# RWKV-7 layer and gated MLP on one core: TensorE's order fixed as emitted in the recurrent layer, and gram groups placed by direction

## The chip, the core and the metric

One core of a Trainium2 chip runs the whole program in one launch. The metric is the device time in microseconds of that execution; lower is better. Five engines matter: TensorE (PE in the profile) multiplies, VectorE (DVE) and ScalarE (ACT) do the elementwise work and empty TensorE's PSUM accumulators, GpSimd (POOL) does a few small operations, and SyncE (SP) issues the loads. Each engine runs its instructions in the order in which they stand in its program; an instruction waits, with all that stand behind it, until the semaphores of its inputs and buffers are set.

## The reference

Input x is 256 tokens of 2048 channels in float32. Two layers follow each other, each adding to its input, with a final norm:

```python
def rwkv7_bidir_mixer(h, ...):                     # layer 0; BRANCH = 4096, 64 heads of 64
    z = h @ w_in                                   # r, k, v, low-rank decay and rate, gate
    zs = zs + mu_prev*(shift_prev(zs)-zs) + mu_next*(shift_next(zs)-zs)
    kk = k*k_k / max(norm(k*k_k), 1e-12)           # per head
    for d, rev in ((0, False), (1, True)):         # two directions in time
        wll = -softplus(-(w0[d] + tanh(dw_d) @ w_up[d])) - 0.5
        decay = exp(-exp(wll))
        a_d = sigmoid(a0[d] + da_d @ a_up[d])
        k_d = k * (1 + (a_d - 1)*k_a)
        y += wkv_scan(r, decay, k_d, v, -kk, kk*a_d, rev)
        # S_t = S_{t-1} diag(w_t) + (S_{t-1} a_t) b_t^T + v_t k_t^T ;  y_t = S_t r_t
        bonus += sum(r*k_d*r_k) * v
    yn = group_norm(y)
    return ((yn + bonus) * silu(gate)) @ w_out

def chunked_sgu_mixer(z, ...):                     # layer 1
    u, v, gate = split(z @ w_in, 3)
    v = layer_norm(gelu(v)); s = w_s @ v (per chunk of 128 and group) + b_s
    return (gelu(u) * s * silu(gate)) @ w_out
```

The change concerns layer 0 alone.

## The kernel before

Each large product is taken in float32 precision by three passes over rounded halves: `mm3` multiplies the high half of the activations by the high half of the weights (line 161), the low half of the activations by the high half of the weights (162), and the high half by the low half (163). Names begin with `acc`; the weights come in 512 KB pieces `raw_*`, which ACT casts to `whi_*` (line 146) and from which DVE subtracts that (`wlo_*`, line 147). Three pieces at most are ahead.

Layer 0 is cut into 16 blocks `b` of two tiles of 128 channels, four heads. The work of a block is spread over three periods of a loop over `p`, and so each period holds work of three blocks:

- `mains(p)`: the projections. In the period of block b, k, r and the low-rank weights `wu` of block b, then v and g of block b-1: `acck`, `accr`, `accv`, `accg`, each 128 by 256 products.
- `factors(p)`: the norm of k (`hs`, line 385; `hb`, line 395; both TensorE), the low-rank products `up` (line 480), whose tanh copies ACT writes to TH and TA (line 482), the cumulated decay SS and its exponentials Et, and from them the factors of the chunked scan: BK (lines 531, 532) and AR (533, 535) on DVE, for both directions `d`, with 64 time steps per chunk, four chunks. `hs`, `hb` and `up` share one PSUM bank ("pf").
- `before(p-1)`: `grams`, the products of BK and AR within each chunk (`gp`, line 557). A gram group is the 8 products of one direction and one channel tile (two heads' halves h, four chunks c; 128 wide, 64 rows each); DVE masks its two banks ("pg", two of them) into Gs (line 562). Then `inverses`, the inverse of a triangular matrix per head and chunk: ACT lays out Dt and NQ (594, 595), DVE takes 31 steps in pairs (610, 612), TensorE makes `qp` (lines 624 and 630).
- `transposed_factors(p-1)`: `bp` (577).
- `after(p-2)`: `values` (`vp`, line 646, copied by ACT to SUV, and AR to RC at line 655), `chain`, four dependent steps i: `xp` and the output products of the state (684, 687), ACT's copy Xs (689), `uu` (693), ACT's copy SUV (695), `sp` and `yp` (700, 702), DVE's new state SJ (707 to 710), ACT's copy of it into SUV (712), which the next step's `xp` reads; last `finish` with the group norm (mv, rs, nm), the bonus `bb` and the transpose `yt` (747).

All these products are small, 64 columns wide or so, and lie between the 128 by 256 products of the projections.

Each of these functions is a generator. It yields the time within the period at which its next piece is to be emitted: a period is nominally `PERIOD` = 78, a step of the chain `CT` = 11 from 9 on, `TSUB` = 50 the end of the 31 steps, `TBT` = 36 the start of `bp`, `TUP` = 43 that of `up`. The loop at the end of the quoted code always advances the generator with the smallest time; that gives the order of emission. From it a scheduler makes the order on each engine: by its own estimates of when an instruction's inputs are there it may place later instructions ahead of earlier ones, and in this loop it does so on all engines. PSUM and SBUF buffers are handed out in emission order.

After the loop layer 0's rest (`oacc`, output projection) and layer 1 follow (`vacc`, `uacc`, `gacc`), which the change doesn't touch.

Of the kernel before, what the change touches and what calls it, by code (L numbers as in the profile page):

```python
# [10 lines left out]
F32 = mybir.dt.float32  # L11
F32R = mybir.dt.float32r
AF = mybir.ActivationFunctionType
ALU = mybir.AluOpType
# [8 lines left out]
def trunk(tc, x, norm_g, final_norm_g, w_in, mu_prev, mu_next, w0, w_up, a0, a_up, k_k, k_a, r_k,  # L23
          ln_w, ln_b, w_out, g_w_in, g_ln_g, g_ln_b, g_w_s, g_b_s, g_w_out, out):
    nc = tc.nc
    V, S, G, PE = nc.vector, nc.scalar, nc.gpsimd, nc.tensor
    P = 128
# [8 lines left out]
    C = 64  # L36
# [12 lines left out]
    raw_pools = [wp]  # L49
    RAW = 1024  # L50

    PERIOD, CT, TSUB, TBT, TEO, TUP = 78.0, 11.0, 50.0, 36.0, 1.2, 43.0
    EB, DK, LAST = 2, 4, 8
    psm = top.enter_context(tc.tile_pool(name="psm", bufs=1, space=PSUM))

    def sm(name, tag="pg", bufs=2):
        return psm.tile([P, 512], F32, tag=tag, name=name, bufs=bufs)
# [352 lines left out]


    MT = PERIOD / 16
    dt = 4 * MT / KT

    def mains(todo, st):
# [29 lines left out]
    def factors(b, f):  # L445
# [20 lines left out]

        PA = sc.tile([P, NC, 2, 2], F32, tag="PA", name=f"PA{b}", bufs=3)
        AR = sc.tile([P, 2, 2, NC, 2, C], F32, tag="AR", name=f"AR{b}", bufs=2)
        yield TUP
        _, wh, wl = f["wu"]  # L470
        ups = []
# [15 lines left out]
        for d in range(2):  # L487
            t = (TUP + 4, PERIOD * 0.7)[d]
            yield t
            th, ta = ups[d]  # L490

            S.activation(th, th, AF.Identity, bias=1.0)
            yield t + 1
            ss = fr.tile([P, 2 * T], F32, tag="SS", name=f"SS{b}_{d}")
            for cl in range(2):
                i0, i1, i2 = ss[:, cl * T:(cl + 1) * T], smask[:, d:d + T], th[:, cl]
                if d == 1:
                    i0, i1, i2 = i0[:, ::-1], i1[:, ::-1], i2[:, ::-1]
                V.tensor_tensor_scan(i0, i1, i2, 0.0, ALU.mult, ALU.add)
            yield t + 2  # L500
            et = fr.tile([P, 2, NC, C + 1], F32, tag="Et", name=f"Et{b}_{d}")
            ef = et.rearrange("p l c t -> p (l c) t")
            sv = ss.rearrange("p (c t) -> p c t", t=C)
            if d == 0:
                G.memset(ef[:, :, 0:1], 1.0)
                e_in, e_ex = ef[:, :, 1:C + 1], ef[:, :, 0:C]
            else:
                G.memset(ef[:, :, C:C + 1], 1.0)
                e_in, e_ex = ef[:, :, 0:C], ef[:, :, 1:C + 1]
            S.activation(e_in, sv, AF.Exp, scale=cE)  # L510
            S.activation(ss, ss, AF.Exp, scale=-cE)
            pe = et[:, :, :, C] if d == 0 else et[:, ::-1, ::-1, 0]
            G.tensor_copy(PA[:, :, d, :], pe.rearrange("p l c -> p c l"))
            yield t + 4

            for cl in range(2):
                j = cts[cl]
                S.activation(th[:, cl], ta[:, cl], AF.Identity, scale=kah[:, j:j + 1], bias=kab[:, j:j + 1])
            eng.tensor_tensor(th, th, Kt, ALU.mult)
            yield t + 6  # L520

            V.scalar_tensor_tensor(ta, ta, 1.0, NK, ALU.add, ALU.mult)

            if d == 0:
                yield PERIOD * 0.6
                BK = se.tile([P, 2, 2, NC, 2, C], F32, tag="BK", name=f"BK{b}")

            def slot(q, natural):
                return scan_order(BK[:, d].rearrange("p l c q t -> p (l c) q t")[:, :, q], d, natural)

            V.tensor_tensor(slot(0, False), tok(ta), sv, ALU.mult)
            eng.tensor_tensor(slot(1, True), tok(th), sv, ALU.mult)
            V.tensor_tensor(scan_order(AR[:, d, :, :, 0].rearrange("p l c t -> p (l c) t"), d), tok(NK), e_ex, ALU.mult)
            yield PERIOD * (0.63, 0.9)[d]
            V.tensor_tensor(scan_order(AR[:, d, :, :, 1].rearrange("p l c t -> p (l c) t"), d, True), tok(f["Rt"]), e_in,
                            ALU.mult)
            KD.append(th)
# [4 lines left out]
        for cl in range(2):  # L542
            V.scalar_tensor_tensor(BQ[:, cl], f["Rt"][:, cl], col["rk"][:, cts[cl]:cts[cl] + 1], KD[0][:, cl],
                                   ALU.mult, ALU.mult)
        f.update(PA=PA, AR=AR, BK=BK, BQ=BQ)

    def grams(b, f):

        AR, BK = f["AR"], f["BK"]
        Gs = sc.tile([P, 2, 16, 2 * C], F32, tag="Gs", name=f"Gs{b}", bufs=2)  # L550
        for d in range(2):
            for cl in range(2):

                gp = [sm(f"gp{b}_{h}{d}{cl}").rearrange("p (c q t) -> p c q t", c=NC, q=2) for h in range(2)]
                for c in range(NC):
                    for h in range(2):
                        PE.matmul(gp[h][:, c].rearrange("p q t -> p (q t)"),  # L557
                                  BK[H[h], d, cl, c].rearrange("p q t -> p (q t)"),
                                  AR[H[h], d, cl, c].rearrange("p q t -> p (q t)"), start=True, stop=True)
                u0 = (d * 2 + cl) * NC  # L560
                for h in range(2):
                    V.tensor_tensor(Gs[:, h, u0:u0 + NC], gp[h].rearrange("p c q t -> p c (q t)"),
                                    gmask[:, d].rearrange("p q t -> p (q t)").unsqueeze(1).to_broadcast([P, NC, 2 * C]),
                                    ALU.mult)
                yield 4 * (d * 2 + cl + 1)
        f["Gs"] = Gs

    def transposed_factors(b, f):
        yield TBT
# [12 lines left out]
    def inverses(b, f):  # L582
# [35 lines left out]
        qp = sm(f"qp{b}", "pq", 1).rearrange("p (u t) -> p u t", t=32)  # L618
        R0 = [slice(h * 64, h * 64 + 32) for h in range(2)]
        R1 = [slice(h * 64 + 32, h * 64 + 64) for h in range(2)]  # L620
        yield TSUB + 3
        for u in range(16):
            for h in range(2):
                PE.matmul(qp[R1[h], u], NQ[R0[h], u], Tn[R0[h], u], start=True, stop=True)
        for h in range(2):
            S.copy(NQ[R1[h]], qp[R1[h]])
        yield TSUB + 5
        for u in range(16):
            for h in range(2):
                PE.matmul(qp[R0[h], u], NQ[R1[h], u], TD[R1[h], u], start=True, stop=True)  # L630
        yield TSUB + 7
        for h in range(2):
            S.copy(TTs[R0[h], h, :, 32:64], qp[R0[h]])
            S.copy(TTs[R0[h], h, :, 0:32], TD[R0[h]])
# [23 lines left out]
    def chain(b, f):  # L658
# [17 lines left out]

        SJ = None
        for i in range(NC):
            t = 9 + CT * i
            yield t  # L680

            xp = part("xp", i)
            for d, l, h, u, suv in each(i):
                PE.matmul(xp[H[h], d * 2 + l], Gs[:, h, u, 0:C], suv, start=True, stop=True)
            if i > 0:
                for d, l, h, u, suv in each(i):
                    PE.matmul(y(d, l, h, i), RC[:, h, u], suv, start=False, stop=False, skip_group_check=True)
            Xs = sc.tile([P, 4, C], F32, tag="Xs", name=f"Xs{b}_{i}")
            S.copy(Xs, xp)
            yield t + CT * 0.27  # L690
            up = part("uu", i)
            for d, l, h, u, _ in each(i):
                PE.matmul(up[H[h], d * 2 + l], TTs[:, h, u], Xs[:, d * 2 + l], start=True, stop=True)
            for h in range(2):
                S.copy(SUV[H[0], :, :, i, h].rearrange("p d l v -> p (d l) v"), up[H[h]])
            yield t + CT * 0.54
            if i < NC - 1:
                sp = part("sp", i)
                for d, l, h, u, suv in each(i):
                    PE.matmul(sp[H[h], d * 2 + l], BT[:, h, u], suv, start=True, stop=True)  # L700
            for d, l, h, u, suv in each(i):
                PE.matmul(y(d, l, h, i), Gs[:, h, u, C:2 * C], suv, start=False, stop=False, skip_group_check=True)
            if i < NC - 1:
                Sn = sc.tile([P, 4, C], F32, tag="SJ", name=f"SJ{b}_{i}", bufs=2)
                pb = PA[:, i].rearrange("p d l -> p (d l)").unsqueeze(2).to_broadcast([P, 4, C])
                if i == 0:
                    V.tensor_tensor(Sn, sp, pb, ALU.mult)
                else:
                    V.tensor_tensor(Sn, sp, SJ, ALU.add)
                    V.tensor_tensor(Sn, Sn, pb, ALU.mult)  # L710
                for h in range(2):
                    S.copy(SUV[H[0], :, :, i + 1, h].rearrange("p d l v -> p (d l) v"), Sn[H[h]])
                SJ = Sn
        f["yp"] = yp

    def finish(b, f):

        tf = 9 + CT * 3.9
        yield tf
        yp, Vt = f["yp"], f["Vt"]  # L720
        st6 = sc.tile([P, 8, 6], F32, tag="st6", name=f"st6_{b}")
# [17 lines left out]
        PE.matmul(bb, ones2.rearrange("p h n -> p (h n)"), f["BQ"], start=True, stop=True)  # L739
        OT = sc.tile([P, 2, T], F32, tag="vy", name=f"OT{b}", bufs=2)  # L740
        V.tensor_tensor(OT, bb, Vt, ALU.mult)
        yield tf + 8
        yt = sm(f"yt{b}", "pc", 1).rearrange("p (l t) -> p l t", l=2)
        for cl in range(2):
            for c in range(NC):
# [10 lines left out]
        nc.scalar.dma_start(oT0[b * 2 * P:(b + 1) * 2 * P].rearrange("(l p) t -> p l t", p=P), OT)  # L756

    def before(b, f):
        yield from grams(b, f)
        yield from inverses(b, f)  # L760

    def after(b, f):
# [115 lines left out]
        oaccs["A"] = oA  # L878

    st = [{} for _ in range(NB)]  # L880
    for p in range(NB + 2):
        act = [mains(plan[p], st) if p <= NB else early_out()]
        if p == 0:
            act.append(low_rank())
        if p < NB:
            act.append(factors(p, st[p]))
        if 0 < p <= NB:
            act += [before(p - 1, st[p - 1]), transposed_factors(p - 1, st[p - 1])]
        if p > 1:
# [2 lines left out]
        while act:  # L892
            cur = min(act, key=lambda a: a[:2])
            try:
                cur[0] = max(cur[0], next(cur[2]))
            except StopIteration:
                act.remove(cur)
    ph.close()

    raw_pools.append(top.enter_context(tc.tile_pool(name="wp2", bufs=2, reuse_waits="tile")))  # L900
# [236 lines left out]
```

## Time and profile before

| | us |
|---|---|
| median of three runs | 2262.61 (2259.36 to 2264.06) |
| the profiled execution | 2260.96 |
| its span in the profile | 2259.2 |
| PE busy in the span | 2210.5 (98%) |
| DVE busy | 1601.3 (71%) |
| ACT busy | 1389.6 (62%) |
| POOL busy | 197.4 (9%) |
| loads | 339.36 MB, mean 150 GB/s |

The mean granted clock of TensorE is 0.992 of full speed. The recurrent layer's loop takes the first 1430 us of the span (the last `yt` starts at 1429.5); from block 4 on `acck` of one block starts 79.2 us after that of the block ahead. The three groups of `acck` products by line number 161, 162 and 163 hold 512 instructions each, 32 for each block. In the window rows each engine's busy time stands with its count of instructions, then the granted clock, the share of the DMA engines and the GB/s. In rows of the timeline the first number is the start, the second the time from the first start to the last end of that run of instructions, and in brackets stands the idle time before it and what ended that.

### The profile page before, as it was taken

What the parts mean: (1) busy time and instruction counts of PE and PEld (TensorE: products, weight loads), DVE (VectorE), ACT (ScalarE), POOL (GpSimd) and SP (SyncE); (2) the same over time, 40 slices, a digit from 0 to 9 for tenths busy, and PEclk for the clock granted to TensorE, in tenths of its full rate; (3) what the DMA queues carried; (4) which work ended last, traced back from release to release, by engine and by line L of the source; (5) the groups of instructions that cost most, each with busy time, mean ns of one, the idle gap of its engine ahead of it and who ended that gap; (6) DMA issues with size and microseconds to landing.
All of it is one profiled execution on the core that took longest, in us unless ns stands there. A gap on an engine that the chain in (4) does not pass through costs nothing.

```text
span 2259.2 us, 50510 instructions
## 1 busy us (share of the span) xinstructions
PE 2210.5 (98%) x21008; PEld 2013.8 (89%) x21008; DVE 1601.3 (71%) x3057; ACT 1389.6 (62%) x2128; POOL 197.4 (9%) x230
## 2 busy tenths in 40 slices
PE   7999999999999999999999999999999999999998
PEld 7898899999999999999999977878889999999886
DVE  5798789778877977887797774465556676676444
ACT  6657777777868777786877774464444444444343
POOL 2220101011111101001110100000000000000000
PEclk9999899999999999999999999999999999999999
DMA  5444234343343344434333455576776666665554
GB/s 167 133 131 136 65 114 123 97 126 117 101 134 107 110 119 125 118 102 130 107 116 117 145 175 171 194 250 193 222 206 188 186 185 189 187 187 189 199 194 156
DMA packets 286135, 339.36 MB, mean 150 GB/s; under 512 B 11600, under 2 KB 233552, under 8 KB 285776
## 3 DMA queue, kind: packets, MB, share of 16 engines
q1 hardware_dynamic: 265648, 314.88, 45.9%
q10 hardware_dynamic: 20256, 21.24, 3.2%
q8 instruction: 165, 2.70, 0.5%
q14 instruction: 66, 0.54, 0.1%
HBM read 329.78 MB, written 6.29 MB: 149 GB/s over the span
## 4 chain that ended last, share of the span: by engine, by line
PE 80%; ACT 8%; DVE 4%; DMA 4%; issue 2%; POOL 0%; SPq 0%; ACTq 0%; POOLq 0%; DVEq 0%
PE oacc L162 4%; PE oacc L163 4%; PE oacc L161 4%; PE gp L557 4%; PE accv L161 3%; PE accg L161 3%; PE uacc L161 3%; PE gacc L163 3%; PE gacc L161 3%; PE gacc L162 3%; PE uacc L162 3%; PE uacc L163 3%; PE accg L163 3%; PE accg L162 3%; PE vacc L163 3%; PE vacc L162 3%
## 5 line engine op out<-in xcount | busy, mean ns | idle before, releaser
L161 PE MATMUL accv<-zh,whi_wv 128*128 128x256 f32 x512 | 153.4, 300 | 2.2 <-ACT whi_wv L146 2.2
L163 PE MATMUL accg<-zh,wlo_wg 128*128 128x256 f32 x512 | 151.3, 295 | 0.5 <-DVE wlo_wg L147 0.5
L161 PE MATMUL acck<-zh,whi_wk 128*128 128x256 f32 x512 | 150.4, 294 | 1.2 <-ACT whi_wk L146 1.2
L163 PE MATMUL acck<-zh,wlo_wk 128*128 128x256 f32 x512 | 148.7, 290 | 2.8 <-DVE wlo_wk L147 2.8
L163 PE MATMUL accv<-zh,wlo_wv 128*128 128x256 f32 x512 | 148.8, 291 | 1.3 <-DVE wlo_wv L147 1.2
L163 PE MATMUL accr<-zh,wlo_wr 128*128 128x256 f32 x512 | 149.2, 291 | 0.6 <-DVE wlo_wr L147 0.6
L162 PE MATMUL accr<-zl,whi_wr 128*128 128x256 f32 x512 | 148.7, 290 | 0.0
L161 PE MATMUL accr<-zh,whi_wr 128*128 128x256 f32 x512 | 148.3, 290 | 0.0
L161 PE MATMUL accg<-zh,whi_wg 128*128 128x256 f32 x512 | 148.0, 289 | 0.0
L162 PE MATMUL accv<-zl,whi_wv 128*128 128x256 f32 x512 | 147.3, 288 | 0.0
L162 PE MATMUL acck<-zl,whi_wk 128*128 128x256 f32 x512 | 147.2, 287 | 0.0
L162 PE MATMUL accg<-zl,whi_wg 128*128 128x256 f32 x512 | 146.4, 286 | 0.0
L162 PE MATMUL uacc<-z1l,whi_u 128*128 128x256 f32 x512 | 146.1, 285 | 0.0
L163 PE MATMUL uacc<-z1h,wlo_u 128*128 128x256 f32 x512 | 146.0, 285 | 0.0
L161 PE MATMUL uacc<-z1h,whi_u 128*128 128x256 f32 x512 | 144.9, 283 | 0.0
L161 PE MATMUL gacc<-z1h,whi_g 128*128 128x256 f32 x512 | 144.9, 283 | 0.0
L162 PE MATMUL gacc<-z1l,whi_g 128*128 128x256 f32 x512 | 144.9, 283 | 0.0
L163 PE MATMUL gacc<-z1h,wlo_g 128*128 128x256 f32 x512 | 144.9, 283 | 0.0
L146 ACT CAST whi_g<-raw_g 128x1024 fp32r<-128x1024 f32 x64 | 67.1, 1048 | 114.0 <-PE uacc L162 73.7
L147 DVE TENSOR_TENSOR wlo_v<-raw_v,whi_v 128x1024 fp32r<-128x1024 f32 x64 | 78.4, 1225 | 80.4 <-ACT whi_v L146 80.4
L610 DVE TENSOR_TENSOR TD<-La,X 128x126 f32<-128x126 f32 (+22 forms) x496 | 126.8, 256 | 10.5
L147 DVE TENSOR_TENSOR wlo_u<-raw_u,whi_u 128x1024 fp32r<-128x1024 f32 x64 | 93.8, 1465 | 56.6 <-ACT whi_u L146 56.6
(333 smaller groups left out, 7307.3 us busy)
## 6 DMA issues: line engine op xcount, KB each, us to landing
raw_wk<-in_rwkv_w_in_dram SPq DMA_DIRECT2D x64, 512.0 KB, 3.9
raw_wr<-in_rwkv_w_in_dram SPq DMA_DIRECT2D x64, 512.0 KB, 3.7
raw_wv<-in_rwkv_w_in_dram SPq DMA_DIRECT2D x64, 512.0 KB, 3.7
raw_wg<-in_rwkv_w_in_dram SPq DMA_DIRECT2D x64, 512.0 KB, 3.7
raw_o<-in_rwkv_w_out_dram SPq DMA_DIRECT2D x64, 512.0 KB, 4.0
raw_v<-in_gmlp_w_in_dram SPq DMA_DIRECT2D x64, 512.0 KB, 4.3
raw_u<-in_gmlp_w_in_dram SPq DMA_DIRECT2D x64, 512.0 KB, 3.6
raw_g<-in_gmlp_w_in_dram SPq DMA_DIRECT2D x64, 512.0 KB, 3.6
```

The source lines that it names most:

```text
L146: latest[0] = S.copy(hi, raw)
L147: latest[1] = V.tensor_tensor(lo, raw, hi.bitcast(F32), ALU.subtract)
L161: PE.matmul(acc, a[0], b[0], start=first, stop=False, skip_group_check=True)
L162: PE.matmul(acc, a[0], b[1], start=False, stop=False, skip_group_check=True)
L163: PE.matmul(acc, a[1], b[0], start=False, stop=last, skip_group_check=True)
L557: PE.matmul(gp[h][:, c].rearrange("p q t -> p (q t)"), BK[H[h], d, cl, c].rearrange("p q t -> p (q t)"), AR[H[h], d, cl, c].rearrange("p q ...
L610: V.tensor_tensor(tv, La[:, j, 0:j].unsqueeze(2).to_broadcast([P, j, n]), X[:, j:j + 1, m:].to_broadcast([P, j, n]), ALU.mult)
```

## The change

Four things are done together. (1) `tc.manual_schedule` is entered for TensorE around the loop: there TensorE's instructions keep the order in which they are emitted, while the other engines' are ordered as before. (2) `grams` is split by direction. The two groups of direction 0 are emitted in the period of `factors`, at 58.1 and 68.1, by `early_grams`; those of direction 1 in the next period, at 8 and 12, right ahead of or behind a small-tile group of the chain. (3) The steps of the chain start at 8 and last 12, with `uu` and `sp` at thirds; the first product `qp` is emitted at 52, the second at 58, `yt` at 68. (4) `TSUB` goes from 50 to 48 and `TBT` from 36 to 41. No instruction's work and no load changes.

```diff
-    PERIOD, CT, TSUB, TBT, TEO, TUP = 78.0, 11.0, 50.0, 36.0, 1.2, 43.0
+    PERIOD, CT, TSUB, TBT, TEO, TUP = 78.0, 12.0, 48.0, 41.0, 1.2, 43.0
...
+    TCH = 8.0
...
+    TGP = ((58.1, 68.1), (TCH, TCH + CT / 3))
+
+    def grams(b, f, d):
...
+        if d == 0:
+            f["Gs"] = sc.tile([P, 2, 16, 2 * C], F32, tag="Gs", name=f"Gs{b}", bufs=2)
+        Gs = f["Gs"]
+        for cl in range(2):
+            yield TGP[d][cl]
...
+    def early_grams(b, f):
+        yield TGP[0][0]
+        yield from grams(b, f, 0)
...
-        yield TSUB + 3
+        yield TCH + CT * 11 / 3
...
-        yield TSUB + 5
+        yield 58
...
-            t = 9 + CT * i
+            t = TCH + CT * i
...
-            yield t + CT * 0.27
+            yield t + CT / 3
...
-            yield t + CT * 0.54
+            yield t + CT * 2 / 3
...
-        tf = 9 + CT * 3.9
+        tf = TCH + CT * 4
...
-        yield tf + 8
+        yield 68
...
-        yield from grams(b, f)
+        yield from grams(b, f, 1)
...
+    fixed = tc.manual_schedule(engines={mybir.EngineType.PE})
+    fixed.__enter__()
...
-            act.append(factors(p, st[p]))
+            act += [factors(p, st[p]), early_grams(p, st[p])]
...
+    fixed.__exit__(None, None, None)
```

What that does to the order of the engines is shown at three places. In the rows the line number stands first, then the operation, the tile that is written, the tiles that are read, the written shape, and a count where rows repeat; the first number in a name is the block.

ACT, in the period in which block 8 runs its chain: from the copy of the first `xp` (Xs, step 0) to the copy of the state for step 1 (SUV from SJ). Dt, NQ and Gs from AR belong to block 9's inverse, the casts and kt to block 10's projections. Before:

```order
L689 COPY Xs8_0_10738<-xp8_0_10729 128x256
L594 COPY Dt9_10826<-Gs9_10623 32x16x32 x2
L595 COPY NQ9_10827<-Gs9_10623 32x512
L695 COPY SUV8_10636<-uu8_0_10752 64x4x64 x2
L594 COPY Dt9_10826<-Gs9_10623 32x16x32 x2
L146 CAST whi_wr10_4_10783<-raw_wr10_4_10781 128x1024
L595 COPY NQ9_10827<-Gs9_10623 32x512
L604 COPY Gs9_10623<-AR9_9963 64x16x64
L146 CAST whi_wr10_8_10858<-raw_wr10_8_10856 128x1024
L374 ACTIVATE kt10_10848<-acck10_10604,c0_174 128x256
L604 COPY Gs9_10623<-AR9_9963 64x16x64
L712 COPY SUV8_10636<-SJ8_0_10816 64x4x64 x2
```

and after:

```order
L700 COPY Xs8_0_10728<-xp8_0_10719 128x256
L605 COPY Dt9_10766<-Gs9_10429 32x16x32 x2
L606 COPY NQ9_10767<-Gs9_10429 32x512
L706 COPY SUV8_10650<-uu8_0_10774 64x4x64 x2
L605 COPY Dt9_10766<-Gs9_10429 32x16x32 x2
L606 COPY NQ9_10767<-Gs9_10429 32x512
L146 CAST whi_wr10_4_10793<-raw_wr10_4_10791 128x1024
L615 COPY Gs9_10429<-AR9_9967 64x16x64 x2
L146 CAST whi_wr10_8_10860<-raw_wr10_8_10858 128x1024
L374 ACTIVATE kt10_10850<-acck10_10631,c0_174 128x256
L723 COPY SUV8_10650<-SJ8_0_10832 64x4x64 x2
```

The same operations stand there, NQ and Gs moved by a place; TensorE's order around them is what differs.

TensorE, at the turn of the period, where block 9's gram groups of direction 1 begin between block 8's `vp` and first chain step and block 10's k projection. Before:

```order
L646 MATMUL vp8_10638<-ident_78,Vt8_10439 128x128 x2
L557 MATMUL gp9_010_10705<-AR9_9963,BK9_10322 128x128
L557 MATMUL gp9_110_10706<-AR9_9963,BK9_10322 128x128
L557 MATMUL gp9_010_10705<-AR9_9963,BK9_10322 128x128
L557 MATMUL gp9_110_10706<-AR9_9963,BK9_10322 128x128
L161 MATMUL acck10_10604<-zh_187,whi_wk10_0_10538 128x256
L162 MATMUL acck10_10604<-zl_188,whi_wk10_0_10538 128x256
L646 MATMUL vp8_10638<-ident_78,Vt8_10439 128x128 x2
```

and after:

```order
L566 MATMUL gp9_010_10707<-AR9_9967,BK9_10335 128x128
L566 MATMUL gp9_110_10708<-AR9_9967,BK9_10335 128x128
L566 MATMUL gp9_010_10707<-AR9_9967,BK9_10335 128x128
L566 MATMUL gp9_110_10708<-AR9_9967,BK9_10335 128x128
L695 MATMUL xp8_0_10719<-SUV8_10650,Gs8_9325 64x64 x8
L161 MATMUL acck10_10631<-zh_187,whi_wk10_8_10634 128x256
L162 MATMUL acck10_10631<-zl_188,whi_wk10_8_10634 128x256
```

The gram group stood in pieces between projections and transposes; after, the group is whole and `xp` follows it directly.

TensorE at the start of the layer, where block 1's k projection (`acck1`) begins. Before:

```order
L163 MATMUL accr0_688<-zh_187,wlo_wr0_12_734 128x256
L161 MATMUL acck1_926<-zh_187,whi_wk1_0_806 128x256
L162 MATMUL acck1_926<-zl_188,whi_wk1_0_806 128x256
L395 MATMUL hb_k0_776<-ident_78,exk0_774 128x128 x4
L163 MATMUL acck1_926<-zh_187,wlo_wk1_0_807 128x256
```

and after:

```order
L566 MATMUL gp0_001_936<-AR0_805,BK0_902 128x128
L566 MATMUL gp0_101_937<-AR0_805,BK0_902 128x128
L566 MATMUL gp0_001_936<-AR0_805,BK0_902 128x128
L566 MATMUL gp0_101_937<-AR0_805,BK0_902 128x128
L161 MATMUL acck1_953<-zh_187,whi_wk1_0_808 128x256
L162 MATMUL acck1_953<-zl_188,whi_wk1_0_808 128x256
L163 MATMUL acck1_953<-zh_187,wlo_wk1_0_809 128x256
```

Block 1's projection began right behind block 0's, ahead of block 0's norm of k; it now begins behind block 0's first two gram groups.

More of the change, by code (lines that the diff above doesn't have):

```diff
@@ L468, in factors @@
         AR = sc.tile([P, 2, 2, NC, 2, C], F32, tag="AR", name=f"AR{b}", bufs=2)
+        f.update(PA=PA, AR=AR)
         yield TUP
@@ L526, in factors @@
                 BK = se.tile([P, 2, 2, NC, 2, C], F32, tag="BK", name=f"BK{b}")
+                f["BK"] = BK
             def slot(q, natural):
@@ L544, in factors @@
                                    ALU.mult, ALU.mult)
-        f.update(PA=PA, AR=AR, BK=BK, BQ=BQ)
-    def grams(b, f):
+        f["BQ"] = BQ
+    TGP = ((58.1, 68.1), (TCH, TCH + CT / 3))
+    def grams(b, f, d):
         AR, BK = f["AR"], f["BK"]
[L550 to L560, printed above, removed]
-                for h in range(2):
[L562 to L566, printed above, removed]
+        if d == 0:
[3 more added lines that the diff above has]
+            yield TGP[d][cl]
+            gp = [sm(f"gp{b}_{h}{d}{cl}").rearrange("p (c q t) -> p c q t", c=NC, q=2) for h in range(2)]
+            for c in range(NC):
+                for h in range(2):
+                    PE.matmul(gp[h][:, c].rearrange("p q t -> p (q t)"),
+                              BK[H[h], d, cl, c].rearrange("p q t -> p (q t)"),
+                              AR[H[h], d, cl, c].rearrange("p q t -> p (q t)"), start=True, stop=True)
+            u0 = (d * 2 + cl) * NC
+            for h in range(2):
+                V.tensor_tensor(Gs[:, h, u0:u0 + NC], gp[h].rearrange("p c q t -> p c (q t)"),
+                                gmask[:, d].rearrange("p q t -> p (q t)").unsqueeze(1).to_broadcast([P, NC, 2 * C]),
+                                ALU.mult)
+    def early_grams(b, f):
+        yield TGP[0][0]
+        yield from grams(b, f, 0)
     def transposed_factors(b, f):
@@ L630, in inverses @@
                 PE.matmul(qp[R0[h], u], NQ[R1[h], u], TD[R1[h], u], start=True, stop=True)
-        yield TSUB + 7
+        yield 60
         for h in range(2):
```

## The prediction

> **What bounds the kernel now.** I read the chain that ended last first, then the windows of one settled period of the recurrent layer, then TensorE's order of time in that period.
>
> ```profile
> PE 80%; ACT 8%; DVE 4%; DMA 4%; issue 2%; POOL 0%; SPq 0%; ACTq 0%; POOLq 0%; DVEq 0%
> ```
>
> ```profile
> 788.50:867.60 79.10, 78.41 (x956) 72.51 (x954) 63.85 (x151) 59.11 (x101) 10.47 (x10) 1.00 0.40 116
> ```
>
> The chain is TensorE's for four fifths, and in the window (PE, PEld, DVE, ACT, POOL, clock, DMA share, GB/s) PE is busy 78.4 of 79.1 us, DVE 64, ACT 59. Eleven such periods of 79.2 follow each other from 305 us on. So PE's own order is the bound, but ACT has 8% of the chain although it is busy only three quarters of the time: it holds PE up at places.
>
> PE pays for changing the size of its tiles:
>
> ```profile
> 807.12 0.28 PE L161 MATMUL accr<-zh,whi_wr 128*128 128x256 f32 x1
> 807.33 0.27 PE L702 MATMUL yp<-SUV,Gs 128*64 128x64 f32 x1
> ...
> 808.46 0.38 PE L162 MATMUL accr<-zl,whi_wr 128*128 128x256 f32 x1
> 808.68 0.28 PE L163 MATMUL accr<-zh,wlo_wr 128*128 128x256 f32 x1
> 808.80 0.28 PE L161 MATMUL accr<-zh,whi_wr 128*128 128x256 f32 x1
> ```
>
> Projection products follow each other at 0.12 us (808.68 to 808.80). Before a small tile it is 0.21, and the first product after one is followed only after 0.22. One excursion costs 0.09 + 0.10 = 0.19 beyond the group itself.
>
> **The change, part by part.** *Fewer excursions.* By the order of one settled period PE leaves the projections 23 times before and 14 times after: 9 x 0.19 = 1.7 us saved a period.
>
> *Whole gram groups.*
>
> ```profile
> 787.85 0.71 PE L557 MATMUL gp<-AR,BK 64*128 64x128 f32 x8
> 788.50 0.38 PE L161 MATMUL acck<-zh,whi_wk 128*128 128x256 f32 x1
> ...
> 789.15 0.48 PE L557 MATMUL gp<-AR,BK 64*128 64x128 f32 x2
> 789.57 1.15 PE L747 MATMUL yt<-ident,yn 128*64 128x64 f32 x32
> ...
> 800.47 1.49 PE L557 MATMUL gp<-AR,BK 64*128 64x128 f32 x16
> 801.89 0.39 PE L161 MATMUL acck<-zh,whi_wk 128*128 128x256 f32 x1
> 802.21 0.69 PE L693 MATMUL uu<-Xs,TTs 128*64 128x64 f32 x16
> ...
> 846.50 0.94 PE L557 MATMUL gp<-AR,BK 64*128 64x128 f32 x12
> 847.37 0.39 PE L161 MATMUL up<-LTh,whi_wu 96*128 96x256 f32 x1
> ```
>
> From start to the next group's start, pieces of 2, 8 and 12 records take 0.42, 0.65 and 0.87, so four records more cost 0.22 when the halves alternate; the 16 of 800.47, with its halves in runs, take 1.42. A whole alternating group is 0.65 + 2 x 0.22 = 1.09. A period has nine pieces now (four of 2, then 6, 8, 12, 14 and 16 records: 4 x 0.42 + 0.64 + 0.65 + 0.87 + 1.09 + 1.42 = 6.35) and then four whole ones (4.36): 2.0 saved. Some four further cuts of xp, yp and sp go, at about 0.2 each: 0.9. PE's own work falls by 1.7 + 2.0 + 0.9 = 4.6 a period.
>
> *The fixed order.* In the order of before a product of the projections stands wherever a small group's input was expected late. Now PE waits for whatever is next as written, and everything behind it waits too. Where do ACT and DVE not keep up? PE is hardly held now:
>
> ```profile
> PE hs_k L385 <- ACT SQ L454: 7.9, 11, 0.8
> ```
>
> That wait, 0.7 a period, stays. New ones, by place:
>
> (a) The second step of the chain. Its xp needs the state that ACT copies (L712). In ACT's new order these stand between the first Xs and that copy: Dt x2, NQ, SUV x2, Dt x2, NQ, a weight cast, Gs x2, a cast, kt, SUV x2, the same operations as before:
>
> ```profile
> 802.52 2.18 ACT L594 COPY Dt<-Gs 32x512 f32<-32x512 f32 x2 [1.96 <-DVE Gs L562]
> 804.72 0.62 ACT L595 COPY NQ<-Gs 32x512 f32<-32x512 f32 x1
> 805.25 0.75 ACT L695 COPY SUV<-uu 64x256 f32<-64x256 f32 x2
> 806.02 2.14 ACT L594 COPY Dt<-Gs 32x512 f32<-32x512 f32 x2
> 808.18 1.05 ACT L146 CAST whi_wr<-raw_wr 128x1024 fp32r<-128x1024 f32 x1
> 809.25 0.62 ACT L595 COPY NQ<-Gs 32x512 f32<-32x512 f32 x1
> 809.90 1.05 ACT L604 COPY Gs<-AR 64x1024 f32<-64x1024 f32 x1
> 810.86 1.04 ACT L146 CAST whi_wr<-raw_wr 128x1024 fp32r<-128x1024 f32 x1
> 811.92 0.47 ACT L374 ACTIVATE kt<-acck,c 128x256 f32<-128x256 f32 x1
> 812.42 1.05 ACT L604 COPY Gs<-AR 64x1024 f32<-64x1024 f32 x1
> 813.49 0.83 ACT L712 COPY SUV<-SJ 64x256 f32<-64x256 f32 x2
> ```
>
> They take 11.8 (802.52 to 813.49 + 0.83) and cannot start until DVE has masked the second gram group, 0.7 after its end (row in (c)). So xp is ready up to 12.5 after that group. In PE's new order there stand only uu (0.7 in the row of 802.21), 24 projections, sp and yp (807.33 to 808.46, 1.1) and 18 projections: 42 x 0.12 + 2 x 0.19 + 0.7 + 1.1 = 7.2. Wait: 5.3 at most. Where all inputs are there ahead of time, ACT's neighbours overlap by some 0.1 (805.25 starts before 804.72 + 0.62); over 15 instructions that is 1.5, so I take 3.8 (bounds 1 and 5.3). In the order of before 45 more products stood between sp and xp, and xp did not wait.
>
> (b) The low-rank products `up` share one PSUM bank, so each waits for two tanh copies of the one ahead.
>
> ```profile
> L655 ACT COPY RC<-AR 64x1024 f32<-64x1024 f32 x2 | 2.1, 1052 | 0.0
> ...
> L482 ACT ACTIVATE TA<-up,pc 128x256 f32<-128x256 f32 x4 | 1.7, 475 | 0.0
> ```
>
> Ahead of the TA copies ACT now has Xs, both RC copies and Et: 0.4 + 2.1 + 0.6, then 0.85 for the two, 3.5 after overlaps. PE has bp (0.36) and 12 products, 1.9, before the third `up`: wait 1.4; the fourth another 0.7. Together 2.1 (0 to 3).
>
> (c) The first direction's grams are written a period earlier, but in the settled order of before they stood there too, between the same projections of r and u; that part of the edit moves little but at the start. What moves on DVE: both BK products, the sum of TH and nm now stand ahead of the third wg subtraction, which before stood ahead of them.
>
> ```profile
> L532 DVE TENSOR_TENSOR BK<-TH,SS 128x512 f32<-128x512 f32 x2 | 1.4, 690 | 0.0
> ...
> L562 DVE TENSOR_TENSOR Gs<-gp,gmask 128x512 f32<-128x512 f32 x8 | 5.2, 687 | 0.8 <-PE gp L557 0.8
> ```
>
> 3 x 0.69 = 2.1 later, nm's wait for POOL beside it, in a stretch where DVE is nearly full: accg waits 1.7 (0 to 3). (d) The second group of direction 1 takes the PSUM banks of the first, whose masks (0.69 each) free them: 0.6.
>
> (e) The first xp waits for four copies from vp, behind a weight cast.
>
> ```profile
> L653 ACT COPY SUV<-vp 64x512 f32<-64x512 f32 x4 | 2.3, 579 | 0.6 <-PE vp L646 0.5
> ```
>
> 2.3 + 1.05 against 18 products and a gram group (3.2): 1.0 with the cast late (0 to 2). (f) In some periods sp waits for uu's copies behind another cast, 0.9 on average (0 to 2.4).
>
> Waits: 3.8 + 2.1 + 1.7 + 0.6 + 1.0 + 0.9 = 10.1; less 4.6: **+5.5 a period, +60 over eleven.** SP's order differs by two w_out loads ten places earlier, late in the layer; POOL's by a memset, one power and the PA copies, by a place or two. The DMAs are the same. No cost: SP and POOL are not in the chain above.
>
> *The start.* In the order of block 0, all 24 `up` products and the first two gram groups now stand ahead of the projections of block 1.
>
> ```profile
> 65.85 0.39 PE L161 MATMUL acck<-zh,whi_wk 128*128 128x256 f32 x1 [0.39 <-ACT whi_wk L146]
> ```
>
> ```profile
> 82.11 1.16 PE L557 MATMUL gp<-AR,BK 64*128 64x128 f32 x15
> ```
>
> Block 1 started at 65.85, block 0's grams at 82.11. If the former must follow the latter, it starts 16 later, and in blocks 1 to 3 the waits above come on top. Bounds 0 (regained later) and 35; I take +25, the 16 and two periods' 5.5. *The end.* Block 15's last period has half the projections (23 us instead of 46) to lie over the same ACT and DVE work, and the output products that filled it now stand where they are written: by the likeness to the start +22 (0 to 35).
>
> *The clock.* PE standing still has slowed its clock in this run:
>
> ```profile
> 95.72 0.68 PE L557 MATMUL gp<-AR,BK 64*128 64x128 f32 x4 [0.94 <-DVE Gs L562]
> ```
>
> ```profile
> 145.00 0.39 PE L163 MATMUL acck<-zh,wlo_wk 128*128 128x256 f32 x1 [1.76 <-DVE wlo_wk L147]
> ```
>
> ```profile
> 252.70 0.58 PE L557 MATMUL gp<-AR,BK 64*128 64x128 f32 x1 [2.87 <-DVE Gs L562]
> ```
>
> ```profile
> 97.90:101.20 3.30, 3.30 (x17) 3.08 (x16) 2.37 (x5) 1.82 (x3) 0.00 (x0) 0.50 0.54 159
> ...
> 251.50:268.50 17.00, 15.80 (x107) 14.88 (x108) 12.03 (x23) 14.37 (x25) 2.40 (x2) 0.50 0.31 94
> ```
>
> After 0.94 and 2.87 us of idleness the granted clock was 0.50 for some 3.4 and 17 us, after 1.76 it was not. At half the clock 3.4 us do the work of 1.7. Only (a) is longer than all but the longest of these; at one in two it adds 0.5 x 1.7 x 14 = 12 (0 to 100, if each of four waits a period did it). The Trainium skill (TensorE: Matmul & The Clock Gate, "Why this matters for your kernels") asks for no idle gap over some 3 us between bursts, since one idle window halves the clock. By that rule (a) alone would do it, in each period: 24 instead of 12; the trace shows shorter waits doing it, and some not.
>
> Sum: 2261.0 (this execution; the median shown is 1.6 higher) + 60 + 25 + 22 + 12 = **2380 us**.
>
> **The rivals.** *ACT and DVE keep up (faster).* The place is (a): if the copies of the state leave ACT before PE has done its 7.2 us, as when Dt and NQ run while the next group is still being multiplied, PE never stands there. With (a) at 0, (b) to (f) at half (3.2), and start and end at 0: 2261 - 11 x 1.4 = 2246; with no wait at all 2261 - 51 = 2210. It decides where the waits fall under 4.6 a period. For it: ACT and DVE are busy 59 and 64 of 79 us, so there is slack to be used. Against it: (a) is the sum of a queue in its written order, which begins at the second masks whatever else is idle. *Gains and waits cancel:* waits of 4.6, start and end regained, 2261. *Half the waits:* 5 a period, start and end 12 each: 2261 + 11 x 0.4 + 24 = 2290. *The clock drops everywhere (slower still).* Four waits a period, each with 3.4 us at half the clock: 2380 - 12 + 100 = 2468. For it: 0.94 us were once enough. Against it: 1.76 were not, and a slow PE gives the others time, so that the next wait shrinks.
>
> **How the numbers follow.** Forecast 0.63; half the waits (2266 to 2310) 0.14; the clock everywhere (2440 to 2500) 0.08; faster 0.12; cancelled 0.03. The forecast's own range is 2310 to 2440: waits of 8 to 13 a period are 23 less to 32 more, start and end of 25 to 70 another 22 less to 23 more. The whole range also takes in the half and ends where the cancelled case ends, at 2265: 0.63 + 0.14 and a part of the rest, 8 in 10. About 0.2% (4.5 us) is what a measurement of this kernel can tell from no change: slower 0.63 + 0.14 + 0.08 = 0.85, same 0.03, faster 0.12.
>
> **What would show it.** The profile after should have gp in whole groups of 16, settled periods of 83 to 87 us, PE waits headed by xp on SUV (3 to 4 us each), then wlo_wg, TA and TH of `up`, and block 1's projections starting near 82. Wrong would be a period under 79, or xp not waiting; then ACT's queue was not the sum I make it.

## The result, and the profile after

The changed kernel takes 2409.11 us, against 2261.45 before. This median of four runs counts one of 3225 us with the clock at 0.60 from end to end; the other three took 2400 to 2416, and the ratio of 1.064 (interval 1.0599 to 1.0681) leaves it out. In a second series it took 2398.41 us, ratio 1.0617 (1.0601 to 1.0633); the profile below is of that series (span 2396.6, clock 0.966). It ran under this expectation:

> The changed kernel again, for a profile at full clock: 2400 to 2415 us. My theory expects settled periods of 84 to 87 us, with TensorE's waits headed by xp on ACT's copy of the state (SUV, 3 to 4 us in most periods), then wlo_wg on DVE, then up on TA and TH, block 1's projections near 82 us, and a granted clock of 1.00 in most of the layer with drops behind the longest waits. The rival that the clock is the loss expects waits no longer than before and stretches at half the clock of 15 us and more in every period.

The time came out 1.6 us below that range. The settled periods (85.4 to 88.2 us) and the wait at their head were about as expected; waits for wlo_wg were not seen, block 1's projections start at 89.0, and the rival's stretches of 15 us at half the clock in every period are not there.

First the chain that ended last of the changed kernel, the line that answers to the first one of before:

```profile
PE 54%; ACT 20%; DVE 14%; DMA 8%; issue 4%; POOL 0%; ACTq 0%; SPq 0%; POOLq 0%; DVEq 0%
```

TensorE's share fell from 80% to 54%; ACT, DVE and loads now hold 42%. The windows by stage, of before (up to block 5's k projection, ten periods of blocks 5 to 14, the layer's end):

```profile
0.00:386.80 386.80, 359.56 (x3812) 339.15 (x3813) 302.01 (x651) 270.71 (x445) 57.94 (x92) 0.96 0.43 124
386.80:1184.40 797.60, 790.41 (x9648) 730.15 (x9646) 644.06 (x1517) 597.72 (x1012) 100.84 (x104) 1.00 0.39 115
1184.40:1514.60 330.20, 324.10 (x2791) 271.08 (x2790) 211.82 (x395) 201.65 (x315) 15.35 (x14) 1.00 0.55 176
```

and of the changed kernel, with one of its periods behind them:

```profile
0.00:428.40 428.40, 361.24 (x3941) 341.79 (x3942) 310.34 (x668) 274.22 (x458) 56.80 (x96) 0.93 0.37 112
428.40:1291.20 862.80, 778.09 (x9542) 726.76 (x9542) 652.58 (x1501) 593.57 (x1001) 70.64 (x100) 0.96 0.35 106
1291.20:1652.00 360.80, 332.67 (x2768) 278.76 (x2767) 213.89 (x394) 201.31 (x313) 11.63 (x14) 0.95 0.50 161
1033.70:1119.30 85.60, 77.61 (x957) 72.57 (x956) 65.25 (x152) 59.29 (x100) 6.74 (x10) 0.96 0.36 108
```

The start lost 41.6 us, the ten periods 65.2, the end 30.6; together 137.4, the whole difference of the spans. In the ten periods TensorE is busy 12.3 us less and idle 77.5 us more (862.80 - 778.09 against 797.60 - 790.41).

The waits of TensorE, whole run, with the total, the count and the longest:

```profile
PE xp L695 <- ACT SUV L723: 68.9, 19, 4.3
PE up L161 <- ACT TA L484: 19.0, 15, 1.4
PE qp L635 <- DVE Tn L627: 13.4, 2, 7.4
PE up L161 <- ACT TH L484: 11.9, 17, 2.1
PE xp L695 <- ACT SUV L664: 11.7, 16, 1.2
...
PE sp L711 <- ACT SUV L706: 9.9, 18, 1.5
```

The two waits of `qp` for DVE's 31 steps are single ones, 7.4 us at the start (142.2 to 149.6) and 6.0 at the end (1432.6 to 1438.5).

The place that carries most, in the order of time of TensorE: gram group and `uu`, then, 12 us on, the wait of the second step's `xp`:

```profile
785.50 1.75 PE L566 MATMUL gp<-AR,BK 64*128 64x128 f32 x16
787.19 0.69 PE L704 MATMUL uu<-Xs,TTs 128*64 128x64 f32 x16
...
799.10 1.43 PE L695 MATMUL xp<-SUV,Gs 128*64 128x64 f32 x15 [4.26 <-ACT SUV L723]
```

ACT over the same time, the rows that answer to the queue shown of before:

```profile
787.81 2.21 ACT L605 COPY Dt<-Gs 32x512 f32<-32x512 f32 x2 [3.82 <-DVE Gs L571]
...
791.32 2.15 ACT L605 COPY Dt<-Gs 32x512 f32<-32x512 f32 x2
...
795.08 2.11 ACT L615 COPY Gs<-AR 64x1024 f32<-64x1024 f32 x2
...
798.65 0.82 ACT L723 COPY SUV<-SJ 64x256 f32<-64x256 f32 x2
```

From the masks to the copy of the state ACT works without a pause, 787.81 to 799.47: 11.7 us. Ahead of that it stood 3.82 us for the masks. With the wait the clock drops; here the drop begins 2.6 us into the wait (794.84 to 799.10) and lasts 6.8:

```profile
797.40:804.20 6.80, 5.10 (x45) 4.84 (x46) 5.72 (x19) 3.80 (x9) 0.00 (x0) 0.50 0.45 137
```

### The profile page after: what moved, and what is told of

The parts are those of the page before. It is cut to its first block, busy times and chain, and to the rows that moved or that the text cites. A ratio compares the mean times of both kernels' runs of the same rounds, so it can differ in the third digit from the quotient of the medians.

```text
span 3223.2 us, 50425 instructions
## 1 busy us (share of the span) xinstructions
PE 3159.1 (98%) x21008; PEld 2766.8 (86%) x21008; DVE 1620.9 (50%) x3057; ACT 1404.6 (44%) x2128; POOL 172.3 (5%) x230
## 4 chain that ended last, share of the span: by engine, by line
PE 92%; ACT 5%; issue 1%; DVE 1%; DMA 0%; SPq 0%; POOL 0%; POOLq 0%; DVEq 0%; ACTq 0%
PE oacc L161 5%; PE oacc L162 5%; PE oacc L163 5%; PE gp L566 3%; PE accr L161 3%; PE accv L161 3%; PE accg L161 3%; PE accg L163 3%; PE accg L162 3%; PE accv L162 3%; PE accv L163 3%; PE accr L163 3%; PE accr L162 3%; PE uacc L163 3%; PE vacc L162 3%; PE uacc L161 3%
## 5 line engine op out<-in xcount | busy, mean ns | idle before, releaser
L161 PE MATMUL accr<-zh,whi_wr 128*128 128x256 f32 x512 | 204.6, 400 | 0.0
L161 PE MATMUL accv<-zh,whi_wv 128*128 128x256 f32 x512 | 200.2, 391 | 0.0
L161 PE MATMUL accg<-zh,whi_wg 128*128 128x256 f32 x512 | 199.5, 390 | 0.0
L161 PE MATMUL acck<-zh,whi_wk 128*128 128x256 f32 x512 | 196.2, 383 | 0.0
L163 PE MATMUL accr<-zh,wlo_wr 128*128 128x256 f32 x512 | 195.1, 381 | 0.0
L162 PE MATMUL accr<-zl,whi_wr 128*128 128x256 f32 x512 | 194.3, 380 | 0.0
L147 DVE TENSOR_TENSOR wlo_wk<-raw_wk,whi_wk 128x1024 fp32r<-128x1024 f32 x64 | 78.4, 1225 | 164.3 <-ACT whi_wk L146 164.3
L146 ACT CAST whi_wk<-raw_wk 128x1024 fp32r<-128x1024 f32 x64 | 67.0, 1047 | 209.6 <-PE accg L162 146.4
L161 PEld LDWEIGHTS accg<-zh,whi_wg 128*128 128x128 f32 x512 | 142.3, 278 | 13.5 <-issue 12.7
L163 PEld LDWEIGHTS accr<-zh,wlo_wr 128*128 128x128 f32 x512 | 151.5, 296 | 0.2
```

The costliest lines, as they stand in the source:

```text
L146: latest[0] = S.copy(hi, raw)
L147: latest[1] = V.tensor_tensor(lo, raw, hi.bitcast(F32), ALU.subtract)
L161: PE.matmul(acc, a[0], b[0], start=first, stop=False, skip_group_check=True)
L162: PE.matmul(acc, a[0], b[1], start=False, stop=False, skip_group_check=True)
L163: PE.matmul(acc, a[1], b[0], start=False, stop=last, skip_group_check=True)
```

## The experiments

### Which part of the change costs: the order or the emission times

The kernel before with the fixed order alone:

```diff
+    fixed = tc.manual_schedule(engines={mybir.EngineType.PE})
+    fixed.__enter__()
     for p in range(NB + 2):
...
+    fixed.__exit__(None, None, None)
```

> The kernel before with TensorE's order fixed as emitted and nothing else changed (its own emission times, grams undivided). My theory, that the fixed order turns late inputs into waits and the emission times only place them: slower than before by about as much as the whole change, 2390 to 2440 us, with hs waiting for SQ by 3 to 4 us a period, xp for SUV and up for TA by 2 each, and gp for Gs by 2. The rival, that the new emission times (grams divided, steps of 12) make the loss: within 1% of before, 2245 to 2285.

The changed kernel with those same three lines taken out:

> The changed kernel without the fixed order: the same emission times and divided grams, but TensorE's instructions ordered by the scheduler as before. My theory: 2255 to 2280 us, within 1% of before, hardly any wait of xp for SUV; the projections fill the places. The rival, that the emission times make the loss: 2370 to 2410.

Measured: fixed order alone 2443.15 us, ratio 1.0821 (1.0803 to 1.0839); new emission times alone 2258.10, ratio 0.9993 (0.9984 to 1.0003). The fixed order makes the whole loss; the emission times, worth nothing without it, make it smaller by 45 us. Waits of TensorE with the fixed order alone:

```profile
PE hs_k L385 <- ACT SQ L454: 56.4, 31, 6.1
PE xp L684 <- ACT SUV L712: 35.2, 15, 2.4
PE up L161 <- ACT TA L482: 30.1, 15, 2.1
```

The same engine is waited for, at other places. My theory was right in kind, and 3 us too low. The start is the fixed order's loss too: with the emission times alone block 5 begins at 386.6, as before (386.8), and not at 428.4. Of the emission times alone, blocks 5 to 14 (first row) and the end (second):

```profile
386.60:1172.70 786.10, 779.04 (x9608) 725.94 (x9607) 647.49 (x1529) 598.22 (x1011) 78.60 (x105) 1.00 0.39 116
...
1172.70:1513.20 340.50, 329.81 (x2929) 274.19 (x2928) 215.08 (x401) 206.95 (x329) 13.29 (x17) 0.99 0.52 171
```

The ten periods gain 11.5 us against before (1.1 each), and the end gives back 10.3.

### The end

The changed kernel with the fixed order left ahead of p = 15:

```diff
-    fixed.__enter__()
     for p in range(NB + 2):
+        if p == 2:
+            fixed.__enter__()
+        if p == 15:
+            fixed.__exit__(None, None, None)
...
-    fixed.__exit__(None, None, None)
```

The edit also enters the fixed order only at p = 2. That did not free the start: TensorE's first 4300 instructions, up to 469 us, stand in the changed kernel's order, and block 1's projection starts at 89.1 as there (89.0). So the run bears on the end alone.

> The changed kernel with the fixed order ended ahead of the last three periods (block 15's gate and value, and the two after it), which are ordered as before. My theory, the term of 22 us for the end: 20 to 27 us less than the changed kernel, all of it behind 1250 us. The rival, that the end is regained anyway since the loads for the next part bound it: within 5 us of the changed kernel.

Measured: 2379.78 us, 18.6 less than the changed kernel, 1.4 short of the range. In its own profile the end falls from 360.8 to 335.6:

```profile
1295.90:1631.50 335.60, 325.10 (x2767) 270.37 (x2766) 210.75 (x393) 201.22 (x313) 16.89 (x14) 0.99 0.54 172
```

So 25 of the 30.6 us lost there are the fixed order's; the rest of the run was 5 us longer, by periods of 84.7 to 89.2 where the changed kernel had 85.4 to 88.2.

### Two edits at the longest wait that gained nothing

Filling TensorE's time ahead of the second `xp`:

```diff
+            for j in range(24 if i == 1 and b < NB - 2 else 0):
+                if j == 0:
+                    xf = sm(f"fill{b}", "pf", 1)
+                PE.matmul(xf[:, :T], zT[0][:, 0, :P], zT[0][:, 0], start=True, stop=True)
             xp = part("xp", i)
```

> The changed kernel, in which TensorE makes 24 more products of 128 by 256 ahead of each second chain step's xp (blocks 0 to 13), into a PSUM bank that nothing reads: 24 x 0.12 = 2.9 us of work more in each of 14 periods, at the place where it stands still for 4.3 us. Theory, that this wait is long enough to halve the clock behind it, 6.8 us at half speed and so 3.4 lost a period: the wait falls to some 1.4 us, no stretch at half the clock follows it, and the time falls by about 14 x 3.4 = 48 to 2340 to 2365 us in spite of the added work. Rival, that the half-speed stretches come from elsewhere (the work behind it, or any wait however short): 2390 to 2405 us, or slower where the added products delay something.

Taking 2.1 us out of ACT's queue:

```diff
         for h in range(2):
-            S.copy(Gs[H[0], h, :, 0:C], AR[H[h], :, :, :, 0].rearrange(...))
+            G.tensor_copy(Gs[H[0], h, :, 0:C], AR[H[h], :, :, :, 0].rearrange(...))
```

> The changed kernel with the two copies from AR into Gs (line 615, 1.05 us each) made by POOL instead of ACT; they stand in ACT's queue ahead of the copy of the state. Theory, that xp's wait is the sum of ACT's queue: it falls from 4.3 to about 2.2, too short to halve the clock, so 2.1 + 3.4 less in each of 14 periods, 77 less, of which a period's next wait (hs on SQ, up on TA) may take back 1 to 2: 2320 to 2350 us. Rival, that xp waits for something else (DVE's new state, PSUM banks): the wait stays at 4, 2385 to 2405 us. Second rival, that POOL is late with the copies, since it has other work: a wait of xp on Gs, over 2400 us.

Measured: 2397.44 (ratio 1.0599, 1.0570 to 1.0627) and 2394.13 (1.0595, 1.0560 to 1.0630); the changed kernel had 1.0617. Both expectations failed, though each edit did at its place what it should. Waits in one period with the filling (771.6 to 857.6):

```profile
PE xp L699 <- ACT SUV L727: 1.4, 1, 1.4
PE hs_k L385 <- ACT SQ L455: 1.1, 1, 1.1
```

and with POOL's copies (774.1 to 860.5):

```profile
PE xp L695 <- ACT SUV L723: 2.1, 1, 2.1
PE xp L695 <- ACT SUV L664: 1.8, 2, 1.2
...
PE hs_k L385 <- ACT SQ L455: 1.3, 1, 1.3
```

The wait fell from 4.3 to 1.4 and to 2.1, as computed. But over the ten periods `hs` now waits 10 to 11 us in all where it waited for nothing, with POOL's copies the first `xp` 18.5 against 6.1; and the ten periods, filled and with POOL's copies, stayed as long:

```profile
430.30:1290.20 859.90, 798.46 (x9783) 747.00 (x9782) 649.67 (x1501) 592.58 (x1000) 67.50 (x100) 0.98 0.35 107
```

```profile
423.70:1290.30 866.60, 785.53 (x9542) 733.99 (x9541) 648.61 (x1501) 572.13 (x981) 90.79 (x120) 0.96 0.35 106
```

The filling kept the clock up in part (0.98 instead of 0.96; 30.7 us of the ten periods at half the clock instead of 64.6). TensorE is busy 20.4 us more there, for 28.8 us of added products (10 x 24 x 0.12), so some 8 us were won, by this estimate; `hs` took back 10. With POOL's copies the clock dropped as much as before (71.7 us), mostly in two short stretches a period. They lie mostly in working time (TensorE busy 3.38 of 3.40 us in one shown at the end), where the changed kernel's lay in part in the wait, and TensorE is busy 7.4 us longer for the same work. My reading is that what waits for what is a loop over several engines, in which a link made shorter shows the next; these two runs fit it but do not prove it.

### Are the loads a link of the loop?

The chain that ended last, in the period from 774.2 us of the changed kernel, at the turn to the next one:

```profile
849.23 0.60 DVE Gs L571
849.83 0.60 DVE BK L534
...
850.82 1.14 DVE wlo_wg L147
851.98 3.52 DMA raw_wk<-in_rwkv_w_in_dram
855.58 1.06 ACT whi_wk L146
```

The subtraction of wg frees a raw buffer, into which the next k weights are loaded, for which ACT stands. ACT's waits for loads in that period, and behind it those of before in one of its periods:

```profile
ACT whi_wk L146 <- DMA raw_wk<-in_rwkv_w_in_dram: 7.1, 4, 2.3
```

```profile
ACT whi_wr L146 <- DMA raw_wr<-in_rwkv_w_in_dram: 4.3, 1, 4.3
...
ACT whi_wk L146 <- DMA raw_wk<-in_rwkv_w_in_dram: 0.6, 2, 0.4
```

In the ten periods of the changed kernel the waits for raw_wk are 4.8 to 8.6 us each, 6.5 on average. ACT stood for loads before the change too, but for those of r and for less: 3.2 us a period (32.3 in ten).

A third raw buffer, in the changed kernel, with POOL's copies as well, and in the kernel before:

```diff
-        return raw_pools[0].tile([P, RAW], F32, tag="raw", name=f"raw_{name}", bufs=2)
+        return raw_pools[0].tile([P, RAW], F32, tag="raw", name=f"raw_{name}", bufs=3)
```

> The changed kernel with three buffers for the weights as loaded (raw) instead of two. New theory, after two edits that took work away from TensorE's wait for ACT and gained nothing: the waits are links of one loop around the turn of the period. The weight subtractions of g come late on DVE, free the raw buffers late, so the loads of the next k weights come late, ACT stands 7.1 us a period in front of their casts, and the copies behind them (vp's, Dt, the state) are late by as much. A third buffer lets the load start one piece sooner: ACT's wait for raw_wk falls from 7.1 to under 2 us a period, the period from 85.7 to 82 to 83.5, the time to 2345 to 2370 us. Rival, that the loop doesn't close over the loads: 2390 to 2405 us with ACT's idle time elsewhere.

> The same with the two copies from AR into Gs made by POOL as well. New theory: with the loads out of the loop, ACT's queue ahead of the copy of the state is what holds xp, and the 2.1 us that gained nothing before now count, with the stretches at half the clock: 20 to 45 us less than with three buffers alone, 2310 to 2340 us. Rival (the copies never matter): within 5 us of it.

> The kernel before with three raw buffers, as the control: its own order puts other products where an input is late, so the loads matter less to it: 2235 to 2260 us, a gain of 0 to 25, half or less of what the changed kernel gains by the same edit. Rival, that the third buffer is worth the same to both (30 us or more): then it says nothing on the fixed order.

Measured: 2380.54 (1.0527, 1.0512 to 1.0543), 2352.89 (1.0400, 1.0383 to 1.0417) and, of the kernel before, 2230.61 (0.9863, 0.9848 to 0.9878). In the changed kernel the third buffer is worth 18 us, 10 short of the low end of what I expected; the kernel before gains 32, its control's rival case. So late loads are no special burden of the fixed order. ACT no longer waits for loads in the ten periods; in one of them (859.5 to 943.9) it now waits at that place for something else,

```profile
ACT whi_wk L146 <- PE accg L162: 3.9, 2, 2.1
```

the `whi` buffers, which TensorE frees. And the periods hardly shrink, 85.7 us where I had put 82 to 83.5:

```profile
427.30:1284.10 856.80, 775.81 (x9543) 728.41 (x9542) 652.46 (x1500) 591.08 (x1000) 72.51 (x100) 0.96 0.35 107
```

That is 6 us in the ten periods; 10.5 of the 18 lie behind them. So the loads alone do not set the period either. With a third buffer POOL's copies count: 27.7 us, within the 20 to 45 expected, where alone they gave 4 (the time itself, 2352.89, lies above the 2310 to 2340 expected, since the third buffer had given less). So the copies lie on the path once the loads don't.

### Several links at once

The changed kernel with POOL's copies and three products moved in the fixed order, two raw buffers:

```diff
-    TGP = ((58.1, 68.1), (TCH, TCH + CT / 3))
+    TGP = ((58.1, 68.1), (8.0, 10.5))
...
-        yield t0 + 2
+        yield t0 + 4
...
-        yield 68
+        yield 72
```

> The changed kernel with POOL's copies into Gs, as before, and three products moved in TensorE's fixed order: the second gram group of direction 1 from 12 to 10.5 (ahead of uu, since ACT stood 3.8 us waiting for its masks), hs from 2 to 4 behind its start, yt from 68 to 72. Two raw buffers. Theory, that the waits are links of a loop over all engines, in which taking one link shorter only shows the next, and several together count: POOL's copies alone gained 4 us, now xp's and hs's waits go below 1 us a period and gp's on Gs comes up to 2: period 81 to 83, 2310 to 2345 us. Rival, that the divided grams or the fixed order cost by something else than these waits: 2380 to 2400 us.

Measured: 2348.25, ratio 1.0390 (1.0373 to 1.0407); 50 us less than the changed kernel, 3 above the range. Ten periods take 823.4 us, and the longest waits are new ones:

```profile
424.70:1248.10 823.40, 765.42 (x9542) 715.11 (x9541) 650.92 (x1501) 571.50 (x980) 93.25 (x120) 0.98 0.39 112
```

```profile
PE sp L712 <- ACT SUV L707: 30.3, 15, 2.4
...
PE up L161 <- ACT TA L485: 20.5, 15, 1.4
PE gp L567 <- DVE Gs L572: 19.8, 16, 3.8
```

Last, all together: three buffers, POOL's copies, the fixed order only from p = 3 to 14, with these times moved, and the same kernel with the scheduler's order:

```diff
+        if p == 3:
+            fixed = tc.manual_schedule(engines={mybir.EngineType.PE})
+            fixed.__enter__()
+        if p == 15:
+            fixed.__exit__(None, None, None)
```

The times moved: TSUB 50, TBT 39.5, TUP 43.5 with `up` every 2.75; the chain's steps at 8.5, 20, 33 and 44, with `uu` 3 and `sp` 7.5 behind; the gram groups at 55.1, 66.6, 8.0 and 10.5; `hs` and `hb` 4 and 10 behind their start; La 18.5, the second `qp` 57, `finish` 54.5 with `bb` 3 behind, `yt` 71.

> As the last, with three raw buffers, the fixed order only from the fourth period (p = 3) to the fifteenth, and smaller moves of up, hb, bb, the first gram groups and the chain's steps. TensorE's work of 74.4 us a period and 1.6 of waiting for uu's copies: period 76, 2200 to 2222 us, below the 2230.6 of the kernel before with three raw buffers. Rival, that the fixed order can at best come out even: 2225 to 2240.

> The last kernel without the fixed order, its emission times and buffers kept: tells what the fixed order itself is worth once its waits are gone. Theory: 2220 to 2240 us, 10 to 20 more than with it, since the small groups are cut again and the projections are left more often. Rival, that the gain is from buffers and emission times alone: the same as with it within 5 us.

Measured: with the fixed order 2257.71, ratio 0.9984 (0.9971 to 0.9997); without it 2228.16, 0.9853 (0.9838 to 0.9868). The expectation for the fixed order failed by 36 us, and the rival, that it comes out even at best, was still too kind. Ten periods of each, fixed and free:

```profile
391.00:1186.80 795.80, 762.30 (x9543) 712.62 (x9542) 647.74 (x1500) 571.56 (x980) 112.09 (x120) 0.99 0.40 115
```

```profile
383.60:1158.30 774.70, 770.16 (x9721) 718.91 (x9719) 648.74 (x1519) 581.53 (x995) 134.05 (x124) 1.00 0.41 119
```

Fixed, TensorE works 0.8 us less a period and stands 2.9 more (33.5 idle against 4.5). The wait left is `sp` on ACT's copies of `uu`, 2.4 us a period where I had put 1.6, followed in six of the periods by a stretch at half the clock:

```profile
PE sp L712 <- ACT SUV L707: 29.1, 12, 2.6
```

The free kernel's time lies in its range, but I had put it 10 to 20 us above the fixed one, and it is 30 below: even with most waits gone the fixed order does not pay. The free kernel equals the kernel before with three raw buffers (0.9863), so the moved times and POOL's copies earn nothing there: of all that was tried, the third buffer is what is worth having, 1.4% on the kernel before.

## Why the prediction was right

2380 was forecast, 2398 to 2409 measured. One reading was off from the start: of the eleven periods of before from 305 us on only nine last 79.2, the first two 81.8 and 85.0. By its own terms, over the ten periods:

- *Work saved, 4.6 a period:* too high. TensorE leaves the projections 30 times in the settled period of before and 22 times in that of after, not 23 and 14, so 8 excursions are saved and not 9. TensorE is busy 12.3 us less in ten periods, in which it also worked about 65 us at half the clock (nine stretches of 6.8 and one of 3.4 among its clock records), busy three quarters of it (5.10 of 6.80 in the row above): some 24 us more than at full clock, by this estimate. So 36 in ten, 3.6 a period.
- *(a), 3.8:* 4.25, as the rows were read, and in three periods a later step's `xp` waits 0.8 to 2.1 more; ACT's queue took 11.7 us, hardly overlapped. *(b), 2.1:* 1.1 to 1.4, and 0.5. *(e) and (f), 1.0 + 0.9:* 0.3 to 1.2 and 0.4 to 1.4.
- *(d), 0.6:* there, in every period, though it is too short for the list of waits. The second gram group of direction 1 takes 1.69 to the next start (785.50 to 787.19 above), the first one 1.09:

```profile
780.52 1.16 PE L566 MATMUL gp<-AR,BK 64*128 64x128 f32 x16
781.61 0.45 PE L695 MATMUL xp<-SUV,Gs 128*64 128x64 f32 x8
```

- *(c), 1.7:* not there. The step that failed is the one from "DVE is late with wg" to "accg waits": accg waits in none of the ten periods, perhaps because up to three pieces of weights are ahead. The raw buffer came free late instead, and ACT stood 6.5 us a period for the next k weights. That this lateness reached TensorE through ACT's copies is argued, not shown: without it the periods were only 0.6 us shorter.
- Waits in all: 7.75 a period more than before (77.5 in ten), where the terms gave 10.1.
- *The clock, 12 in all:* mis-sized. Each 4.3 us wait came with a drop, of 6.8 us in nine periods of ten, where one of 3.4 in every second period was put: 24 us in these ten periods, double the whole term. The Trainium skill (TensorE: Matmul & The Clock Gate, "Why this matters for your kernels") asks for no idle gap over some 3 us. That rule came nearer here: the trace agrees for the wait of 4.25, though half-clock stretches followed waits of 1.1 to 2.4 us as well.
- Together 7.75 + 2.4 - 3.6 = 6.5 a period, where 5.5 stood, with the clock apart.
- *Start 25 and end 22:* 41.6 and 30.6, clock drops included. Block 1's projection started at 89.0, not near 82, and behind it come two waits that no term had, `hs` for SQ (6.1) and `qp` (7.4); at the end `qp` waits 6.0. That the fixed order makes the end's loss is shown by the run that frees it, that it makes the start's by the run with the emission times alone; which of the waits counts there was not tried.

The sum came close since work saved and waits were both put too high, and clock and start too low. What the experiments add is that the waits do not add up as the prediction took them: the largest were right in their places, yet taking half or more of the largest away gave nothing that the measurement tells from none. Whether they close a loop, and over which links, was not settled, only that ACT's copies count once a third raw buffer is there.

## What to carry to other kernels

A fixed order turns each input that comes late into a wait for all that stands behind it, so it pays only where every group's input is early by a margin; here the work saved was 3.6 us a period and the waits 7.75. Before removing the longest wait, follow what made its producer late: here shortening one wait brought up others, and in the changed kernel only several edits together moved the periods by more than 1 us. Try the cheap buffer first: the third raw buffer was worth more than any order that was tried.

## What the hardware showed

The clock drops in whole stretches of 3.4 us. In the ten periods, after 4.25 us of idleness it was two of them (6.8 us) in nine of ten. With POOL's copies there were two single ones in most periods, here one behind the 2.1 us wait of `xp` and one behind the 1.1 us wait of `hs`:

```profile
1142.32 1.44 PE L695 MATMUL xp<-SUV,Gs 128*64 128x64 f32 x15 [2.12 <-ACT SUV L723]
...
1148.29 0.61 PE L385 MATMUL hs_k<-bones,SQ 128*128 128x2 f32 x4 [1.08 <-ACT SQ L455]
```

```profile
1142.40:1145.80 3.40, 3.38 (x37) 3.08 (x38) 3.05 (x11) 1.54 (x4) 0.00 (x0) 0.50 0.63 198
1149.20:1152.60 3.40, 3.40 (x28) 3.06 (x27) 3.04 (x13) 1.25 (x3) 1.67 (x1) 0.51 0.50 154
```

So the length of one wait does not tell what follows: waits of 2.4 us (the last fixed kernel) were followed by a drop in six periods of ten, and in two periods of the filled kernel a drop of 10.2 us followed a wait of 1.4.

The drop may be no fixed price either: while TensorE is slow, ACT and DVE can catch up, and part of it may come back where the next wait is for them. No run here isolates that. The filled kernel has the clock at 0.98 and its ten periods at 860 us against 863, but it also does the added products.
